# Second SwiGLU product in a written-down order: plain part last, operands stored split, first operands and weights fetched during the first product

## The chip, the cores and the metric

The kernel runs on one core of a Trainium2 chip. The metric is the device time of one execution in microseconds (us); several executions are timed and the median is taken. The engines of the core are TensorE (PE, with its weight loads PEld), VectorE (DVE), ScalarE (ACT), GpSimd (POOL) and SyncE (SP). SP issues nearly all DMA transfers of this kernel, in one queue, in the order in which the program writes them.

## What is computed

One inference step of a decoder with two layers, for a prompt of 1024 tokens and 32 sample tokens, all in fp32, D_MODEL 1024, D_FF 2816. Layer 0 mixes tokens with sliding-window attention, layer 1 with a recurrent block. Both layers end in the same SwiGLU part, which is what the change is about:

```
def swiglu(h, w_in, w_out):
    g, u = jnp.split(h @ w_in, 2, axis=-1)
    return (jax.nn.silu(g) * u) @ w_out
...
xp = xp + swiglu(rms_norm(xp, ffn_norm[layer]), w_ffn_in[layer], w_ffn_out[layer])
```

Below, "the first product" is `h @ w_in` with the SiLU gate behind it, and "the second product" is the multiplication by `w_out` with its addition to x. After layer 0 comes the norm of the recurrent block, after layer 1 the final norm, whose results `y0`, `y1`, `y2` are outputs.

## The kernel before, in words

**Arithmetic.** A fp32 matmul is done as three matmuls of a split form: every operand is held as a high part (rounded) and a low part (the rest), and `mm3` (its matmuls are on L309) adds high·high, high·low and low·high. So each matrix block, weight or activation, must be split before TensorE can use it: one ACT instruction writes the high part, one DVE subtraction the low part.

**Tokens.** The 1056 tokens lie transposed (features on partitions) in three tiles of 384, 384 and 288 columns, called t = 0, 1, 2. The residual x of a tile is held in two SBUF tiles of four feature blocks each (`x[t][0]` for blocks 0 to 3, `x[t][1]` for 4 to 7).

**First product.** D_FF is cut into 22 blocks f. For f = 0 and 1 each tile is computed plainly (`h_in`). For f = 2 to 21 the tiles 0 and 1 are computed together by `seven`, a Strassen-like scheme with seven block products in place of eight (84 matmuls of 384 columns), and tile 2 plainly by `h_in` (48 matmuls of 288 columns). During this the residual x lies in DRAM (`xd`), to make room. The hidden activations go to DRAM too: for every odd f, `keep_pair` forms the sums that the second product needs, splits six blocks and stores the high and low part of each (12 DMAs to `od`, L897 and L898). Each of these stores waits for its ACT and DVE instruction, and everything behind it in SP's queue waits with it.

**Second product.** It has a plain part, for the hidden blocks 0 and 1 (`h_out`, 144 matmuls), and 20 units (`unit`), for 5 chunks c of four hidden blocks times 4 pairs mp of output blocks. A unit is again seven products for tiles 0 and 1, in banks A, B and Dk, 42 matmuls of 384 columns, and for tile 2 24 plain matmuls of 288 columns. A unit needs nine stored operands of its chunk (b11, b21, b22, t1 to t4, and two for tile 2), a split weight block w, and the split sums ws of that weight (`Mix` on POOL, four instructions on L156 to L159, then `MixSums`). Every product that ends is added to x by DVE (`add`, L1022); a bank that goes on accumulating waits for the DVE instruction that has just read it.

**Order before.** TensorE's and SP's instructions stay in program order; ACT, DVE and POOL are ordered by a scheduler. `ffn_phase` (L838) builds a list of items; `drive` (L283) runs it, and after each item prepares what comes next in the list of needs as far as there is room. Room is scarce: 18 SBUF slots in one pool and 6 in another (`hs`) hold normalized inputs, sums, x and operands; six slots hold weights. In the second product the order before is: reload x into SBUF (`reload`, called after block f = 18), rest of the first product, plain part (`outs`), 20 units (`mixed`), of which those of the last chunk leave out tile 2, and last the tile 2 part of that chunk, with the norm of tiles 0 and 1 between (`rest`). The operands of the first chunk are fetched when the slots of the first product are free, during the plain part.

Of the kernel before, what the change touches and what calls it, by code (L numbers as in the profile page):

```python
# [9 lines left out]
OP = mybir.AluOpType  # L10
# [56 lines left out]
class Weight:  # L67


    def __init__(self, src, ext=False, place=None):  # L70
        self.src, self.ext, self.place, self.t, self.slot, self.raw = src, ext, place, None, None, None

    def prep(self, k, early=False):
        nc = k.nc
        ok = [s for s in k.wslots.free if self.ext or s[0] is k.gw]
        raw = ok and (self.place() if self.place else k.gw.tile([P, 1024], F32, name=k.nm("raw"), tag="raw", bufs=NRAW))
        if not raw:
            return False
        self.raw = raw
        self.slot = ok[0]  # L80
        k.wslots.free.remove(self.slot)
        nc.sync.dma_start(raw, self.src)
# [42 lines left out]
class Hidden:  # L125


    def __init__(self, hd, ch, t, slots, pool):
        self.hd, self.ch, self.tile, self.slots, self.pool, self.t, self.slot = hd, ch, t, slots, pool, None, None

    def prep(self, k):
        if not self.slots.free:
            return False
        W = WID[self.tile]
        self.slot = self.slots.get()
        raw = k.gw.tile([P, 2, W], F32, name=k.nm("raw"), tag="raw", bufs=NRAW)
        k.nc.sync.dma_start(raw, self.hd[self.ch, self.tile])
        self.t = self.pool().tile([P, 2, 2, WMAX], F32R, name=k.nm("h"), tag=self.slot)
        k.split(self.t[:, :, 0, :W], self.t[:, :, 1, :W], raw)
        return True  # L140

    def free(self, k):
        self.slots.put(self.slot)


class Mix:


    def __init__(self, w):
        self.w, self.t = w, None  # L150

    def prep(self, k):
        r = self.w.raw
        a, b, c, d = (r[:, i * 256:(i + 1) * 256] for i in range(4))
# [5 lines left out]
        self.t = r  # L160
        return True


class MixSums:


    def __init__(self, w):
        self.w, self.t, self.slot = w, None, None

    def prep(self, k):  # L170
        if not k.wslots.free:
            return False
        self.slot = k.wslots.get()
        self.t = self.slot[0].tile([P, 2, 1024], F32R, name=k.nm("w"), tag=self.slot[1])
# [1353 lines left out]
```

## Time and profile before

| | us |
|---|---|
| median of 3 runs (2188.15 to 2189.56) | 2188.75 |
| the profiled execution, its own time | 2185.0 |
| span in its trace | 2183.2 |
| PE busy in the span | 2129.7 (98%) |
| DVE busy | 1494.8 (68%) |
| ACT busy | 1010.0 (46%) |
| POOL busy | 243.0 (11%) |

The span of the trace leaves out 1.8 us of the profiled execution's time; the medians of the timed runs are 3.75 us above that execution. PE's busy time counts a matmul from its issue to its modelled end, so that a stream of matmuls without a gap is 100% busy whatever its rate; what matters is where PE is not busy, and which wait ends there.

### The profile page before, as it was taken

The page shows a single profiled execution, that of the slowest core. Times are in us where ns is not written, and L with a number is a line of the kernel's source. Part 1 is how long each engine was busy: PE and PEld are TensorE (multiplying, and loading weights), DVE is VectorE, ACT ScalarE, POOL GpSimd, SP SyncE. Part 2 cuts the span into 40 slices and gives each one's busy share as a digit, 9 for nine tenths or more (in the row PEclk, how much of TensorE's full clock was granted, in tenths as well). Part 3 has the DMA queues.
Part 4 walks back from the last instruction along what each step waited for, and adds up shares of the span by engine and source line. Part 5 has one row for each costly group of instructions (what it writes and reads, how often), then busy time and mean ns, then how long its engine had stood idle before and what let it go on. Part 6 is the DMA issues. An engine that isn't in the chain of part 4 may idle for free.

```text
span 2183.2 us, 35146 instructions
## 1 busy us (share of the span) xinstructions
PE 2129.7 (98%) x13608; PEld 2097.9 (96%) x13608; DVE 1494.8 (68%) x2936; ACT 1010.0 (46%) x1835; POOL 243.0 (11%) x328
## 2 busy tenths in 40 slices
PE   9999999999999999999999989999999999999997
PEld 9899989999999999999999989999999999999996
DVE  6877786756656666566776788787656666676666
ACT  5666655434444443112258887754444444422123
POOL 1223230000000001133100000000000000024222
PEclk9999999999999999999999999999999999999998
DMA  5332334323243355856112123441343343685442
GB/s 193 101 105 79 121 119 157 98 103 132 101 153 123 125 205 182 317 232 228 50 58 67 60 68 116 136 167 65 113 156 119 114 149 124 222 320 199 187 157 80
DMA packets 129135, 305.77 MB, mean 140 GB/s; under 512 B 13960, under 2 KB 82120, under 8 KB 128968
## 3 DMA queue, kind: packets, MB, share of 16 engines
q1 hardware_dynamic: 128208, 303.21, 39.9%
q8 instruction: 106, 1.74, 0.3%
q14 instruction: 61, 0.50, 0.1%
q10 hardware_dynamic: 760, 0.33, 0.1%
HBM read 220.99 MB, written 84.49 MB: 140 GB/s over the span
## 4 chain that ended last, share of the span: by engine, by line
PE 79%; DVE 10%; ACT 4%; DMA 4%; POOL 2%; issue 2%; SPq 0%; POOLq 0%; DVEq 0%; ACTq 0%
PE mm L309 75%; DVE w L88 2%; DMA o<-od 2%; DVE x L1022 1%; ACT w L84 1%; PE pt L628 1%; DVE w L348 1%; PE s L580 1%; DVE s L598 1%; DVE xn L348 1%; ACT s L605 1%; ACT w L347 0%; DVE x L423 0%; DMA raw<-in_wz 0%; POOL x L1384 0%
## 5 line engine op out<-in xcount | busy, mean ns | idle before, releaser
L309 PE MATMUL mm<-xn,w 128*128 128x384 f32 (+1 forms) x5808 | 927.0, 318 | 9.3 <-DVE w L88 3.8
L309 PEld LDWEIGHTS mm<-xn,w 128*128 128x128 f32 x5808 | 902.1, 188 | 14.2 <-DVE w L88 4.5
L309 PE MATMUL mm<-o,w 128*128 128x384 f32 (+1 forms) x2640 | 430.1, 323 | 11.8 <-DVE x L1022 8.8
L309 PEld LDWEIGHTS mm<-o,w 128*128 128x128 f32 x2640 | 420.7, 188 | 19.8 <-DVE x L1022 15.4
L88 DVE TENSOR_TENSOR w<-raw,w 128x1024 fp32r<-128x1024 f32 x246 | 300.0, 1225 | 131.6 <-ACT w L84 130.3
L84 ACT ACTIVATE w<-raw 128x1024 fp32r<-128x1024 f32 x248 | 261.3, 1056 | 199.2 <-PE mm L309 59.6
L309 PE MATMUL mm<-T,w 128*128 128x384 f32 x1920 | 351.5, 338 | 1.0 <-ACT sg L990 0.5
L309 PEld LDWEIGHTS mm<-T,w 128*128 128x128 f32 x1920 | 338.8, 188 | 1.8 <-ACT sg L990 1.1
L1022 DVE TENSOR_TENSOR x<-mm,x 128x384 f32<-128x384 f32 (+1 forms) x416 | 213.3, 531 | 134.2 <-PE mm L309 133.3
L156 POOL TENSOR_TENSOR raw<-raw 128x256 f32<-128x256 f32 x40 | 30.8, 771 | 1191.6 <-DMA raw<-in_wz 462.1
L347 ACT ACTIVATE w<-raw 128x1024 fp32r<-128x1024 f32 x40 | 42.5, 1062 | 259.8 <-PE mm L309 134.3
L620 POOL TENSOR_SCALAR s<-s,sm 128x256 f32<-128x256 f32 (+1 forms) x128 | 83.5, 669 | 210.2 <-DVE sm L618 96.3
L309 PE MATMUL mm<-att,w 128*128 128x384 f32 (+1 forms) x576 | 97.5, 325 | 0.0
L309 PEld LDWEIGHTS mm<-att,w 128*128 128x128 f32 x576 | 91.7, 188 | 1.9
L309 PE MATMUL mm<-y,w 128*128 128x384 f32 (+1 forms) x576 | 93.5, 322 | 0.0
L309 PEld LDWEIGHTS mm<-y,w 128*128 128x128 f32 x576 | 92.4, 188 | 0.0
L605 ACT ACTIVATE s<-s,sm 128x256 f32<-128x256 f32 (+1 forms) x128 | 61.7, 483 | 46.4 <-DVE sm L602 46.4
L364 ACT ACTIVATE sq<-x 128x384 f32<-128x384 f32 (+1 forms) x105 | 51.0, 491 | 56.9 <-DVE x L1022 39.6
L895 ACT ACTIVATE hi<-e 128x384 fp32r<-128x384 f32 x80 | 41.8, 522 | 69.7 <-DVE e L1013 33.7
L117 DVE TENSOR_TENSOR w<-raw,w 128x1024 fp32r<-128x1024 f32 x40 | 48.9, 1223 | 35.9 <-ACT w L115 35.8
L348 DVE TENSOR_TENSOR w<-raw,w 128x1024 fp32r<-128x1024 f32 x40 | 49.6, 1240 | 19.9 <-ACT w L347 19.7
L997 ACT ACTIVATE sg<-sg 128x384 f32<-128x384 f32 x40 | 21.0, 525 | 90.8 <-DVE sg L996 90.8
(211 smaller groups left out, 2367.4 us busy)
## 6 DMA issues: line engine op xcount, KB each, us to landing
o<-od SPq DMA_DIRECT2D x70, 768.0 KB, 9.4
od<-hi SPq DMA_DIRECT2D x140, 192.0 KB, 2.0
raw<-in_wg SPq DMA_DIRECT2D x44, 512.0 KB, 4.1
raw<-in_wu SPq DMA_DIRECT2D x44, 512.0 KB, 5.1
raw<-in_wz SPq DMA_DIRECT2D x40, 512.0 KB, 7.8
od<-e SPq DMA_DIRECT2D x80, 192.0 KB, 2.0
raw<-in_wq SPq DMA_DIRECT2D x24, 512.0 KB, 3.6
raw<-in_wo SPq DMA_DIRECT2D x24, 512.0 KB, 3.6
```

The lines of the kernel that those rows point to most:

```text
L84: nc.scalar.activation(self.t[:, 0, :], raw, AF.Copy)
L88: nc.vector.tensor_tensor(self.t[:, 1, :], raw, self.t[:, 0, :].bitcast(F32), OP.subtract)
L117: tt(d[:, 1, :], g, d[:, 0, :].bitcast(F32), OP.subtract)
L156: tt(d, c, d, OP.add)
L309: mm = lambda *a, **k: self.nc.tensor.matmul(*a, skip_group_check=more, **k)
L347: nc.scalar.activation(hi, src, AF.Copy)
L348: nc.vector.tensor_tensor(lo, src, hi.bitcast(F32), OP.subtract)
L364: nc.scalar.activation(sq[:, :W], self.xview(t, kb), AF.Square)
L605: nc.scalar.activation(s[:, j, :N], s[:, j, :N], AF.Exp, bias=sm[:, 1, j:j + 1], accum_out=sm[:, 3, j:j + 1])
L620: nc.gpsimd.tensor_scalar(s[:, j, :N], s[:, j, :N], sm[:, 4, j:j + 1], 1.0, op0=OP.mult, op1=OP.mult)
L895: nc.scalar.activation(hi.bitcast(F32R), src, AF.Copy)
L1022: tt(x, ps[:, :WID[t]], x, OP.add)
```

## The change

It concerns the second product of both layers, and small things beside it.

1. The plain part moves from before the units to behind them (`h_out`, tiles 0, 1, 2), and gives the norms of tiles 0 and 1 their place: their steps are called inside `h_out` of tiles 1 and 2 at chosen output blocks m. All 20 units now have the same form, with tile 2 in them.
2. The hidden blocks 0 and 1 are stored split, as two parts (`keep`), where before they were stored whole and split after the load.
3. What the second product needs first is fetched during the first: `lead` is woven between the last four items of the first product. y are the two items of f = 20 (`seven`, then tile 2), z those of f = 21.
4. `reload` of x moves from behind f = 18 to behind `seven` of f = 21, and takes the halves x[0][0], x[1][0], x[2][0] first.
5. In the units the loads, splits and adds come at written places: `steps[0]` behind the third product, `steps[1]` behind the fourth. There DVE's adds and the two splits are pinned to program order. `drive` no longer skips ahead to operands; a gate holds back the next phase's weights.
6. The small instructions between the sum of squares and the spread of the norm get a high priority. Of the eight stores of `y2`, four are issued by ACT.

The core of the diff:

```diff
-    def unit(w, ws, o, mp, fin, hh=None):
-        b11, b21, b22, t1, t2, t3, t4 = o
+    def unit(w, ws, o, mp, steps):
+        b11, t3, b21, t2, h0, h1, t4, t1, b22 = o
...
         prod(B, w, 1, b21, True)
-        add(0, m0, B, fin)
+        add(0, m0, B)
+        steps[0]()
         prod(A, ws, 0, t2, False)
         add(0, m1, A)
-        if hh:
-            plain(w, hh, m0, False)
+        steps[1]()
+        plain(w, (h0, h1), m0)
         prod(Dk, w, 3, t4, False)
...
     def reload():
         for t in range(NT):
             self.xt[t] = [self.act_tile([P, 4, WMAX], F32, "x") for _ in range(2)]
-            for i in range(2):
+        for i in range(2):
+            for t in range(NT):
                 nc.sync.dma_start(self.xt[t][i][0][:, :, :WID[t]], self.xd[t][:, 4 * i:4 * i + 4, :])
...
+        lead = [[lambda: fetch(0, 0, 6)], [lambda: do(0, "load")],
+                [lambda: do(0, "parts"), lambda: do(0, "sums"), lambda: do(1, "load")],
+                [reload, lambda: fetch(0, 6, 9), lambda: do(1, "parts"), lambda: do(2, "load")], [lambda: pin(True)],
+                [lambda: pin(False)]]
...
+            def s0(u=u, c=c, mp=mp):
+                if mp < 3 and c + 1 < NCH:
+                    fetch(c + 1, 3 * mp, 3 * mp + 3)
+                if mp < 3 and c + 1 == NCH:
+                    assert H[mp].prep(self)
+                do(u + 1, "sums")
+                do(u + 3, "load")
+                gate.open = u == n - 1
+            st = (s0, lambda u=u: do(u + 2, "parts"))
...
+        steps = [{}, {2: n0[1:2], 5: n0[3:4]}, {1: n1[1:2], 4: n1[3:4]}]
...
-        for f in range(NPL, NF):
+        for f in range(NPL, NF - 2):
             L += blocks(f)
-            if f == NF - 4:
-                L.append(reload)
-        p = outs()
-        m, q = mixed()
-        L += p
-        for i, x in enumerate(m):
+        y, z = blocks(NF - 2), blocks(NF - 1)
+        L += lead[0] + [y[0]] + lead[1] + [y[1]] + lead[2] + [z[0]] + lead[3] + [z[1]] + lead[4]
+        for i, x in enumerate(units):
...
-        L += [q[0]] + n0[1:2] + [q[1]] + n0[3:] + [q[2]] + n1[1:2] + [q[3]] + n1[3:]
+        L += lead[5] + p[:2] + n0[4:] + [p[2]] + n1[4:]
```

In it `load` starts the DMA of a weight block, `parts` splits it and then mixes it in place on POOL, and `sums` splits the mixed block; n0 and n1 are the steps of the norms of tiles 0 and 1 ([1] the sum over partitions, [3] the spread, [4:] the application).

**First place: SP's queue at the end of the first product of layer 0, before.** The first rows are the last stores of `keep_pair` for f = 21 (`od`, from `hi` and from `e` or `t`); x has long been loaded.

```order
L898 DMA od_4823<-e_1162_8909 128x384
L897 DMA od_4824<-hi_9256 128x384
L898 DMA od_4824<-t_9227 128x384
L195 DMA o_9314<-od_4782 128x1536
L195 DMA o_9316<-od_4783 128x1536
L195 DMA o_9318<-od_4784 128x1536
L195 DMA o_9320<-od_4785 128x1536
L195 DMA o_9322<-od_4786 128x1536
L195 DMA o_9324<-od_4787 128x1536
L195 DMA o_9326<-od_4788 128x1536
L195 DMA o_9328<-od_4789 128x4x288
L195 DMA o_9330<-od_4790 128x4x288
```

The same place in the change, from the same three stores on; `x` from `xd` is the reload, the three `o` are t4, t1 and b22 of the first chunk, `raw` from `in_wz` is the weight block of the third unit.

```order
L894 DMA od_4823<-e_1168_8933 128x384
L893 DMA od_4824<-hi_9251 128x384
L894 DMA od_4824<-t_9222 128x384
L965 DMA x_9256<-xd_71 128x1536
L965 DMA x_9258<-xd_72 128x1536
L965 DMA x_9260<-xd_73 128x4x288
L965 DMA x_9257<-xd_71 128x1536
L965 DMA x_9259<-xd_72 128x1536
L965 DMA x_9261<-xd_73 128x4x288
L202 DMA o_9268<-od_4788 128x1536
L202 DMA o_9270<-od_4785 128x1536
L202 DMA o_9272<-od_4784 128x1536
```

Six of the nine operands have left this place (they are now ahead of the stores of f = 20), the six loads of x have come to it, and both still stand behind the twelve stores of f = 21. The next row of the change is `L149 DMA raw_9281<-in_wz 128x1024`.

**Second place: DVE in the first unit of layer 0, before.** `x` from `mm` are the adds, `w` from `raw` the low parts of weights; `w_9406` is the split of the third unit's weight block, `raw_9404`.

```order
L1022 TENSOR_TENSOR x_8680<-mm_9567,x_8680 128x384
L1022 TENSOR_TENSOR x_8684<-mm_9569,x_8684 128x384
L1022 TENSOR_TENSOR x_8680<-mm_9568,x_8680 128x384
L1022 TENSOR_TENSOR x_8680<-mm_9567,x_8680 128x384
L1022 TENSOR_TENSOR x_8688<-mm_9598,x_8688 128x288
L1022 TENSOR_TENSOR x_8680<-mm_9569,x_8680 128x384
L1022 TENSOR_TENSOR x_8684<-mm_9567,x_8684 128x384
L88 TENSOR_TENSOR w_9406<-raw_9404,w_9406 128x1024
L1022 TENSOR_TENSOR x_8688<-mm_9626,x_8688 128x288
```

And in the change; `w_9385` is the split of the third unit's weight block, `raw_9281`, and bank A is `mm_9343`.

```order
L1014 TENSOR_TENSOR x_9256<-mm_9343,x_9256 128x384
L1014 TENSOR_TENSOR x_9258<-mm_9345,x_9258 128x384
L1014 TENSOR_TENSOR x_9256<-mm_9344,x_9256 128x384
L135 TENSOR_TENSOR w_9373<-raw_9118,w_9373 128x1024
L1014 TENSOR_TENSOR x_9256<-mm_9343,x_9256 128x384
L135 TENSOR_TENSOR w_9385<-raw_9281,w_9385 128x1024
L1014 TENSOR_TENSOR x_9260<-mm_9392,x_9260 128x288
L1014 TENSOR_TENSOR x_9256<-mm_9345,x_9256 128x384
L1014 TENSOR_TENSOR x_9258<-mm_9343,x_9258 128x384
L1014 TENSOR_TENSOR x_9260<-mm_9420,x_9260 128x288
L1014 TENSOR_TENSOR x_9258<-mm_9343,x_9258 128x384
```

The split of the third unit's weight has moved ahead of three adds of the first unit, the third of which (bank A to x of tile 1) TensorE's seventh product waits for.

**Third place: POOL at the end of the kernel, before.** `rc` is the inverse root of the norm of a tile, tiles 0, 1, 2 in turn; `x` times `rs` is the final norm applied to tile 1 (eight blocks) and to two blocks of tile 2.

```order
L377 TENSOR_TENSOR rc_21860<-rc_21860,mhalf 128x3
L377 TENSOR_TENSOR rc_21959<-rc_21959,mhalf 128x3
L377 TENSOR_TENSOR rc_22032<-rc_22032,mhalf 128x3
L1384 TENSOR_TENSOR x_19141<-x_19141,rs_22014 128x384 x4
L1384 TENSOR_TENSOR x_19142<-x_19142,rs_22014 128x384 x4
L1384 TENSOR_TENSOR x_19145<-x_19145,rs_22047 128x288
L1384 TENSOR_TENSOR x_19146<-x_19146,rs_22047 128x288
```

And in the change:

```order
L379 TENSOR_TENSOR rc_21833<-rc_21833,mhalf 128x3
L379 TENSOR_TENSOR rc_21941<-rc_21941,mhalf 128x3
L1384 TENSOR_TENSOR x_19722<-x_19722,rs_21995 128x384 x4
L1384 TENSOR_TENSOR x_19723<-x_19723,rs_21995 128x384 x4
L379 TENSOR_TENSOR rc_22046<-rc_22046,mhalf 128x3
L1384 TENSOR_TENSOR x_19724<-x_19724,rs_22061 128x288
L1384 TENSOR_TENSOR x_19725<-x_19725,rs_22061 128x288
```

The inverse root of tile 2 now stands behind the eight multiplications of tile 1.

More of the change, by code (lines that the diff above doesn't have):

```diff
@@ L75, in prep @@
         ok = [s for s in k.wslots.free if self.ext or s[0] is k.gw]
[L76 to L77 removed]
+        if not ok:
             return False
[L79 removed]
         self.slot = ok[0]
         k.wslots.free.remove(self.slot)
+        raw = self.raw = k.gw.tile([P, 1024], F32, name=k.nm("raw"), tag="raw", bufs=NRAW)
         nc.sync.dma_start(raw, self.src)
@@ L122, in free, with __init__, fill, load @@
             k.wslots.put(s)
[L125 to L140, printed above, removed]
-    def free(self, k):
[L143 to L154, printed above, removed]
+class Part:
+    def __init__(self):
+        self.t, self.slot = None, None
+    def fill(self, k, raw):
+        nc, pin = k.nc, k.tc.keep_in_program_order if k.pinned else lambda x: x
+        self.slot = k.wslots.get()
+        self.t = self.slot[0].tile([P, 2, 1024], F32R, name=k.nm("w"), tag=self.slot[1])
+        pin(nc.scalar.activation(self.t[:, 0, :], raw, AF.Copy))
+        pin(nc.vector.tensor_tensor(self.t[:, 1, :], raw, self.t[:, 0, :].bitcast(F32), OP.subtract))
+    def free(self, k):
+        k.wslots.put(self.slot)
+class Mixed:
+    def __init__(self, src):
+        self.src, self.w, self.s = src, Part(), Part()
+    def load(self, k):
+        self.raw = k.gw.tile([P, 1024], F32, name=k.nm("raw"), tag="raw", bufs=NRAW)
+        k.nc.sync.dma_start(self.raw, self.src)
+    def parts(self, k):
+        self.w.fill(k, self.raw)
+        a, b, c, d = (self.raw[:, i * 256:(i + 1) * 256] for i in range(4))
         tt = k.nc.gpsimd.tensor_tensor
@@ L159, in prep, with sums, __init__, parts @@
         tt(b, b, a, OP.subtract)
[L160 to L168, printed above, removed]
-    def prep(self, k):
[L171 to L174, printed above, removed]
-        k.split(self.t[:, 0, :], self.t[:, 1, :], self.w.raw)
-        return True
-    def free(self, k):
-        k.wslots.put(self.slot)
+    def sums(self, k):
+        self.s.fill(k, self.raw)
+class Whole:
+    def __init__(self, src):
+        self.src, self.w = src, Part()
+    load = Mixed.load
+    def parts(self, k):
+        self.w.fill(k, self.raw)
+    def sums(self, k):
+        pass
+class Gate:
+    def __init__(self):
+        self.t, self.open = None, False
+    def prep(self, k):
+        return self.open
 class Operand:
@@ L846, in ffn_phase @@
         T, HD_, OD = {}, {}, {}
-        late = []
+        n0, n1 = after
+        pools = [(lambda: self.hp, hs), (lambda: self.gp, self.slots)]
         NCH = (NF - 2) // 4
@@ L924, in h_in @@
             u = self.proj(wu, self.xn[t], W)
-            flush()
             if last:
@@ L1033, in h_out, with plain @@
                              h[:, c, 0, :W], h[:, c, 1, :W], c == 0, c == 1)
-                add(t, m, ps)
-        def plain(w, hh, m, fin):
+                x = self.xview(t, m)
+                with tc.high_priority(PRI):
+                    tt(x, ps[:, :W], x, OP.add)
+                if l == 1 or t < 2:
+                    self.square(t, m)
+                for fn in steps.get(m, ()):
+                    fn()
+        def plain(w, hh, m):
             W = WID[2]
@@ L1092, in blocks @@
                     Item(lambda a, b: h_in(a, b, f, 2, last=f == NF - 1), w, w)]
-        def outs():
-            w = [Weight(I[f"wd{l}"][k], True) for k in range(2)]
-            h = [Hidden(HD_, 0, t, hs, lambda: self.hp) for t in range(NT)]
-            return [Item(lambda a, b, h, t=t: h_out(a, b, h, t), w + [h[t]],
-                         (w if t == 2 else []) + [h[t]]) for t in range(NT)]
-        def third():
-            if "raw" not in T:
-                if not hs.free:
-                    return None
-                T["raw"] = hs.free.pop()
-            t = self.hp.tile([P, 4 * WMAX], F32, name=self.nm("raw"), tag=T["raw"])
-            return t[:, :1024]
```

115 lines of the change are left out of this document (50 added, 65 removed).

## The prediction

> **What bounds the kernel now.** I read the page first (busy times, then the costliest groups), then who waits for whom on PE, then PE's busy time over the two second products, then the timelines of PE and SP around their starts and ends.
>
> ```profile
> PE 2129.7 (98%) x13608; PEld 2097.9 (96%) x13608; DVE 1494.8 (68%) x2936; ACT 1010.0 (46%) x1835; POOL 243.0 (11%) x328
> ...
> L88 DVE TENSOR_TENSOR w<-raw,w 128x1024 fp32r<-128x1024 f32 x246 | 300.0, 1225 | 131.6 <-ACT w L84 130.3
> L84 ACT ACTIVATE w<-raw 128x1024 fp32r<-128x1024 f32 x248 | 261.3, 1056 | 199.2 <-PE mm L309 59.6
> ...
> L1022 DVE TENSOR_TENSOR x<-mm,x 128x384 f32<-128x384 f32 (+1 forms) x416 | 213.3, 531 | 134.2 <-PE mm L309 133.3
> ```
>
> PE works without a break nearly everywhere: 53.5 us of 2183.2 are not busy. The change leaves the number of matmuls as it is, so it can only move PE's waits and the stretch behind its last matmul. A weight's split costs 1.06 us on ACT and 1.22 us on DVE, an add to x 0.53 us.
>
> PE's longest waits, by what ended them (us, times, longest),
>
> ```profile
> PE mm L309 <- DVE x L1022: 8.8, 18, 2.5
> ```
>
> and PE's busy time from the first to the last matmul of the units, layer 0 and layer 1:
>
> ```profile
> 880.40:1103.90 223.50, 216.62 (x1340) 212.14 (x1338) 147.52 (x249) 50.84 (x61) 55.05 (x74) 1.00 0.51 191
> 1943.20:2164.30 221.10, 216.20 (x1340) 212.20 (x1339) 147.36 (x250) 54.92 (x70) 59.85 (x75) 1.00 0.48 182
> ```
>
> The units lose 6.9 and 4.9 us to waits, mostly for an add that a weight's split holds up on DVE. That is all that a better order inside them can win: 11.8 us.
>
> PE around the start of the second product of layer 0 (T and xn belong to the first product, h to the plain part, o to the units):
>
> ```profile
> 838.50 4.39 PE L309 MATMUL mm<-T,w 128*128 128x384 f32 x24
> 842.72 2.24 PE L309 MATMUL mm<-xn,w 128*128 128x384 f32 x12
> ...
> 849.03 8.60 PE L309 MATMUL mm<-xn,w 128*128 128x384 f32 x60
> 857.47 23.15 PE L309 MATMUL mm<-h,w 128*128 128x384 f32 x144
> 880.46 1.22 PE L309 MATMUL mm<-o,w 128*128 128x384 f32 x6
> ```
>
> From start to start, 24 matmuls of 384 columns take 842.72 - 838.50 = 4.22 us, so 0.176 each. The row at 849.03 holds the last 12 of `seven` for f = 21 and 48 of tile 2. I call the end of `seven` E: 849.03 + 12 x 0.176 = 851.1. Tile 2 then covers 6.3 us and the plain part 23.0 us, before the first unit needs its operands.
>
> SP in the same stretch, from the last store of f = 21 on:
>
> ```profile
> 866.80 1.41 SPq L898 DMA_DIRECT2D od<-t  x1
> 868.30 5.29 SPq L195 DMA_DIRECT2D o<-od  x9
> ```
>
> The store leaves at E + 15.7, and only then the nine operands, at E + 17.2. For f = 19 a row of PE and one of SP:
>
> ```profile
> 806.79 10.71 PE L309 MATMUL mm<-xn,w 128*128 128x384 f32 x72
> ```
> ```profile
> 820.87 0.44 SPq L898 DMA_DIRECT2D od<-t  x1
> ```
>
> There `seven` ended at 806.79 + 2.1 = 808.9, and the last store left 12.0 us behind it.
>
> How long the nine operands take, from the chain of waits, their sizes, and the load of the DMA engines meanwhile:
>
> ```profile
> 873.06 14.08 DMA o<-od
> ```
> ```profile
> o<-od SPq DMA_DIRECT2D x70, 768.0 KB, 9.4
> ...
> o<-od SPq DMA_DIRECT2D x20, 576.0 KB, 13.1
> ...
> x<-xd SPq DMA_DIRECT2D x8, 768.0 KB, 6.5
> ...
> x<-xd SPq DMA_DIRECT2D x4, 576.0 KB, 10.9
> ```
> ```profile
> 870.00:890.00 20.00, 18.83 (x120) 18.09 (x119) 10.86 (x21) 1.85 (x2) 0.00 (x0) 1.00 1.02 407
> ```
>
> Seven of 768 KB and two of 576 KB need 887.1 - 868.3 = 18.8 us from the first issue to the last landing. The DMA engines are full (share 1.02), at 407 GB/s: 1.9 us for 768 KB, 1.3 us for a weight block of 512 KB.
>
> **The change part by part.**
>
> *Start of the units, the term that decides.* The plain part no longer stands between E and the units: they begin at E + 6.3. In SP's queue the twelve stores of f = 21 still come first, then six loads of x (four of 768 KB, two of 576 KB), then t4, t1 and b22: by the sizes above exactly the bytes of the nine operands of before. What was hidden under 29.3 us now lies under 6.3.
>
> When does SP get past the stores? Before, at E + 17.2, with splits of hidden blocks and weights among the stores' instructions; at f = 19, at 12.0. Those splits go, but two weight splits come, and each high part's buffer waits for an earlier store to land. I take E + 11, with 17 as one end; the other end is DVE's own work on these blocks, 13 instructions (five sums, six low parts, two of tile 2) at the price of this row:
>
> ```profile
> L896 DVE TENSOR_TENSOR e<-e,hi 128x384 fp32r<-128x384 f32 x16 | 9.1, 586 | 2.0 <-ACT hi L895 2.0
> ```
>
> 13 x 0.59 = 7.6 us. From E + 11, counted back from the last landing at + 18.8 by 1.9 us per 768 KB and 1.4 per 576 KB: x of tile 0 lands at E + 15.3, t4 at E + 26.0, b22 at E + 29.8, the third weight block at E + 31.1.
>
> A matmul of 288 columns takes (1096.04 - 1092.77) / 24 = 0.136 us:
>
> ```profile
> 1092.77 3.43 PE L309 MATMUL mm<-o,w 128*128 128x288 f32 x24
> 1096.04 0.22 PE L390 MATMUL mm<-idr,rh 128*128 128x128 f32 x1
> ```
>
> PE in the first unit: three products of 6 x 0.176 = 1.06 us end at E + 9.5. The fourth goes on in bank A and needs the first add, so x: 15.3 + 0.5 = E + 15.8, a wait of 6.3. It and half of tile 2 (12 x 0.136 = 1.6) bring PE to E + 18.5; the fifth needs t4: 26.0, a wait of 7.5. Fifth, sixth and the other half of tile 2 bring it to E + 29.7. The seventh needs the add of bank A, which on DVE stands behind the split of the third weight block: 31.1 + 1.06 + 1.22 and three adds of 0.53 make E + 35.0, a wait of 5.3. Sum: 19.1 us per layer, **+38.2**. With SP free at 7.6 or 17 it is 15.7 or 25 per layer. From then on a unit of 42 x 0.176 + 24 x 0.136 = 10.7 us needs a quarter of a chunk's operands and one weight block, 18.8 / 4 + 1.3 = 6 us of DMA, so I expect no further wait.
>
> What the clock does after a wait is in PE's rows and the stretch of the change of layers:
>
> ```profile
> 1107.67 0.47 PE L390 MATMUL mm<-idr,rh 128*128 128x128 f32 x1 [3.76 <-DVE rh L378]
> ...
> 1110.16 20.13 PE L309 MATMUL mm<-xn,w 128*128 128x384 f32 x107
> ```
> ```profile
> 1100.00:1120.00 20.00, 15.35 (x86) 14.93 (x85) 18.34 (x41) 10.13 (x19) 0.85 (x1) 0.83 0.17 52
> ```
>
> *Clock.* Behind a wait of 3.8 us the granted clock of these 20 us is 0.83, and 107 matmuls take 20.1 us where 107 x 0.176 = 18.8: 1.3 us lost. The waits above are longer; what two of them cost is covered by the next wait, the third is not: 2 x 1.3, **+2.6** (0 to 6). [...]
>
> *Inside the units.* The written order puts each add ahead of the split that used to hold it up, and gives banks tile 2's 1.6 us as cover in the last chunk too: the waits of before go, **-11.8** (at least -9). What is late next is nothing on DVE: a unit has 9 adds and 2 splits, about 7 of 10.7 us.
>
> *Change of layers.* Before, 4.7 us of waits in the 20 us from 1100 on, and 1.3 of clock. In the change the sums and spreads of both norms lie inside `h_out`, with high priority. But DVE still has 16 instructions of the norm of tile 0 and six adds to do after the second sum, 22 x 0.53 = 11.7 us against six blocks of tile 2, 6 x 6 x 0.136 = 4.9, of matmuls left, and the recurrent block's first matmuls follow it: I leave 2 us of wait. **-4** (0 to -6). Inside `h_out` DVE has an add and a sum of squares per 1.06 us of PE, so each sum over partitions may wait half a us: **+1**.
>
> *Tail.* Rows of before:
>
> ```profile
> 2160.85 3.43 PE L309 MATMUL mm<-o,w 128*128 128x288 f32 x24
> ```
> ```profile
> 2167.87 0.85 POOL L377 TENSOR_TENSOR rc<-rc,mhalf 128x3 f32<-128x3 f32 x1 [3.56 <-DVE rc L376]
> 2168.69 9.16 POOL L1384 TENSOR_TENSOR x<-x,rs 128x384 f32<-128x384 f32 x10
> ...
> 2172.43 2.64 DVE L1386 SCALAR_TENSOR_TENSOR x<-x,vec,mm 128x288 f32<-128x288 f32 x6 [1.79 <-ACT rs L397]
> ```
>
> The last product ends at 2164.3, the span 18.9 us later, with POOL's ten multiplications (0.92 us each) as the last link. In the change eight of them start some 2 us before PE's end, since the spread of tile 1 lies three output blocks (3 x 6 x 0.136 = 2.4 us) ahead of it, so they end about 6 us behind it. The inverse root of tile 2 now queues behind them, 3 us later than before, but then only two are left: root at + 6.8, DVE's last product as before 6.4 us later (2175.07 - 2168.72), a store and its landing, which I put at 2: about + 15. **-4** (0 to -6).
>
> *At nothing:* the split storing of blocks 0 and 1 adds six ACT and six DVE instructions per layer early in the first product, where PE's stream hides them (3.5 us of DVE if it did not); the six early operands take 10.5 us of DMA during two items of 21 us each, and the weights of f = 21 stand ahead of them in SP's queue.
>
> Sum: 38.2 + 2.6 - 11.8 - 4 + 1 - 4 = +22.0. The profiled execution took 2185.0 us (1.8 outside its span), so 2207.0 by its measure; its median stands 3.75 above: 2188.75 + 22.0 = **2210.75 us**.
>
> **The rivals.**
>
> 1. *The queue is free in time* (faster). If the twelve stores left by E, because nothing but their own splits stands in ACT and DVE, every landing above comes 11 us earlier and a layer loses 8.1 us at the start: 2188.75 + 22.0 - 22.0 = 2188.75. That is the point from which it decides; at E - 3 it gives about 2183. For it: the blocks' splits have less beside them than before. Against it: the last at + 12.0 and + 15.7, and 7.6 us of DVE work. Faster needs this or a landing that my sizes don't give: 0.14. Between, within 0.2% (4.4 us, about what a measurement of this kernel can tell from no change): 0.06.
> 2. *The start's delay stays.* If the third and fourth weight blocks land late too, since each is queued behind three operands, DVE's pinned order stops PE again in the second unit, by a block's 18.8 - 11 = some 5 us per layer: 2221 or more. For it: share 1.02 for 40 us. Against it: 6 of 10.7 us of DMA are enough for a unit. 0.06.
> 3. *The change does not fetch early enough to matter, nor late enough to hurt*: SP free at 7.6 and all gains at their best ends: 31.4 - 11.8 - 6 - 6 = +8, 2196. 0.14.
>
> My forecast has the rest, 0.60. In all: faster 0.14, same 0.06, slower 0.80. The range leaves out rival 2 (0.06) and most of rival 1: 2188 to 2221.
>
> **What would show it.** Right: three waits of PE in the first unit of each layer, ended by the add of x, by DMA of o, and by an add of bank A with a weight's split ahead of it; SP's x loads about 11 us behind `seven`; units without waits afterwards; a shorter tail. Wrong: x loaded within a few us of E, or PE in step through the first unit. If the first unit takes less than 19 us (10.7 and 8.1), the sign of the forecast falls.

## The result, and the profile after

| | before | changed |
|---|---|---|
| median of 4 runs each (range), us | 2188.45 (2186.22 to 2189.56) | 2211.30 (2210.47 to 2212.06) |
| the profiled execution, us | 2185.0 | 2210.95 |
| span in its trace, us | 2183.2 | 2208.9 |
| mean granted clock | 0.99 | 0.983 |

The changed kernel takes 1.0106 of the time of before (95% interval 1.0088 to 1.0123): 22.85 us more by the medians, where +22.0 was forecast. By the spans it is 25.7 us more, mostly since the profiled execution of before lay 3.4 us under its median and that of the change only 0.35. L numbers are now those of the changed kernel: L310 the matmuls, L1014 the add to x in a unit, L1026 that in `h_out`, L366 the sums of squares.

First who waits for whom on PE: the total, the number of waits, the longest.

```profile
PE mm L310 <- DVE x L1014: 24.6, 4, 9.9
PE mm L310 <- DMA o<-od: 10.4, 2, 5.3
PE mm L373 <- DVE acc L366: 10.0, 3, 7.5
```

Before, the add to x ended 18 waits of 2.5 us at most. Now it ends four long ones, two in each layer, and the operands `o` end one in each. PE around the start of the units, layer 0:

```profile
847.76 8.60 PE L310 MATMUL mm<-xn,w 128*128 128x384 f32 x60
...
868.54 4.78 PE L310 MATMUL mm<-o,w 128*128 128x384 f32 x18 [9.00 <-DVE x L1014]
878.45 5.98 PE L310 MATMUL mm<-o,w 128*128 128x384 f32 x24 [5.12 <-DMA o<-od]
887.01 28.16 PE L310 MATMUL mm<-o,w 128*128 128x384 f32 x155 [2.58 <-DVE x L1014]
```

E, the end of `seven` for f = 21, is 847.76 + 12 x 0.176 = 849.87. Behind it come tile 2, three products, and then the three forecast waits. The fourth product starts at 868.54, E + 18.7; the fifth, which needs t4, at E + 28.6; the seventh, which needs the add of bank A, at E + 37.1. The rows also show the clock: 18 matmuls (6 of 384 columns, 12 of 288) take 4.78 us where 6 x 0.176 + 12 x 0.136 = 2.7 are due, the next 24 take 5.98 instead of 3.7. The granted clock of these two stretches was 0.56 and 0.62.

That the seventh product waits behind the third weight block shows on DVE, which has the block's split directly ahead of four adds (885.58 to 887.32), among them that of bank A:

```profile
884.43 1.23 DVE L135 TENSOR_TENSOR w<-raw,w 128x1024 fp32r<-128x1024 f32 x1 [11.98 <-ACT w L134]
```

Layer 1:

```profile
1919.20 8.60 PE L310 MATMUL mm<-xn,w 128*128 128x384 f32 x60
...
1940.90 4.53 PE L310 MATMUL mm<-o,w 128*128 128x384 f32 x18 [9.92 <-DVE x L1014]
1950.74 5.76 PE L310 MATMUL mm<-o,w 128*128 128x384 f32 x24 [5.32 <-DMA o<-od]
1959.56 25.68 PE L310 MATMUL mm<-o,w 128*128 128x384 f32 x157 [3.06 <-DVE x L1014]
```

E is 1919.20 + 2.11 = 1921.31, and the same three products start at E + 19.6, 29.4 and 38.3. What SP does meanwhile in layer 0, with the last of the twelve stores, the x tiles, and t4, t1 and b22:

```profile
862.95 0.32 SPq L894 DMA_DIRECT2D od<-t  x1
863.37 3.49 SPq L965 DMA_DIRECT2D x<-xd  x6
866.90 1.60 SPq L202 DMA_DIRECT2D o<-od  x3
```

The x loads leave at E + 13.5, behind the stores. Then the units from the seventh product of the first one to the end of the twentieth, in each layer, and the first 6 us of that stretch in layer 0 (length; busy time of PE, PEld, DVE, ACT, POOL; granted clock, DMA share, GB/s):

```profile
887.01:893.00 5.99, 5.99 (x19) 5.99 (x20) 1.43 (x3) 1.28 (x2) 1.72 (x3) 0.50 1.02 423
887.01:1091.00 203.99, 203.99 (x1261) 203.99 (x1262) 130.43 (x209) 38.31 (x38) 51.85 (x71) 0.98 0.56 199
1959.56:2160.50 200.94, 200.94 (x1260) 200.94 (x1261) 130.43 (x209) 37.35 (x37) 51.83 (x71) 1.00 0.51 185
```

PE is busy for the whole of both: the waits of 6.9 and 4.9 us that the units had before are gone. The same work takes 3.05 us more in layer 0, since the clock was still at 0.50 behind the third wait there; in layer 1 it was at 1.00. At the change of layers, PE's rows with a wait:

```profile
1111.50 0.83 PE L373 MATMUL mm<-ones,acc 128*128 128x1 f32 x6 [0.45 <-DVE acc L366]
...
1120.90 1.15 PE L310 MATMUL mm<-xn,w 128*128 128x384 f32 x5 [0.36 <-DVE xn L349]
1122.45 0.44 PE L310 MATMUL mm<-xn,w 128*128 128x384 f32 x1 [0.40 <-ACT xn L348]
1123.26 7.07 PE L310 MATMUL mm<-xn,w 128*128 128x384 f32 x39 [0.37 <-DVE xn L349]
```

1.6 us of waits in all, and the 39 matmuls of the last row run at the full rate (39 x 0.176 = 6.9), where before there were 4.7 us and a granted clock of 0.83; from 1100 to 1120 it is now 1.00. Last the tail, all engines, with PE's last 18 matmuls of the plain part in the first row:

```profile
2187.72 2.61 PE L310 MATMUL mm<-o,w 128*128 128x288 f32 x18
...
2188.49 9.00 POOL L1384 TENSOR_TENSOR x<-x,rs 128x384 f32<-128x384 f32 x8 [4.11 <-ACT rs L399]
...
2189.62 1.18 DVE L366 TENSOR_TENSOR acc<-acc,sq 128x288 f32<-128x288 f32 x1
2190.72 0.44 DVE L1026 TENSOR_TENSOR x<-mm,x 128x288 f32<-128x288 f32 x1
...
2192.26 5.55 DVE L366 TENSOR_TENSOR acc<-acc,sq 128x288 f32<-128x288 f32 x5
...
2197.86 1.44 PE L373 MATMUL mm<-ones,acc 128*128 128x1 f32 x6 [7.53 <-DVE acc L366]
```

The last of them ends at 2190.33 and the span 18.6 us later, against 18.9 before. While POOL multiplies tile 1, DVE's sums of squares of tile 2 take about 1.1 us each, and PE waits 7.53 us for them.

### The profile page after: what moved, and what is told of

The parts are those of the page before. It is cut to its first block, busy times and chain, and to the rows that moved or that the text cites. A ratio compares the mean times of both kernels' runs of the same rounds, so it can differ in the third digit from the quotient of the medians.

```text
span 2208.9 us, 35229 instructions
## 1 busy us (share of the span) xinstructions
PE 2133.2 (97%) x13608; PEld 2107.0 (95%) x13608; DVE 1496.0 (68%) x2934; ACT 1008.7 (46%) x1841; POOL 237.1 (11%) x328
## 4 chain that ended last, share of the span: by engine, by line
PE 82%; DVE 8%; ACT 4%; DMA 3%; issue 1%; POOL 1%; SPq 0%; ACTq 0%; DVEq 0%; POOLq 0%
PE mm L310 79%; DMA raw<-in_wz 1%; DVE w L87 1%; PE pt L630 1%; ACT w L83 1%; PE s L582 1%; DVE s L600 1%; ACT s L607 1%; DVE acc L366 1%; DMA x<-xd 1%; DVE xn L349 0%; PE mm L373 0%; DVE pr L349 0%; ACT w L134 0%; DVE xs L425 0%
## 5 line engine op out<-in xcount | busy, mean ns | idle before, releaser
L310 PE MATMUL mm<-xn,w 128*128 128x384 f32 (+1 forms) x5808 | 927.2, 318 | 11.7 <-DVE w L87 3.8
L310 PEld LDWEIGHTS mm<-xn,w 128*128 128x128 f32 x5808 | 900.8, 188 | 18.2 <-DVE w L87 4.7
L310 PE MATMUL mm<-o,w 128*128 128x384 f32 (+1 forms) x2928 | 482.6, 327 | 35.0 <-DVE x L1014 24.6
L310 PEld LDWEIGHTS mm<-o,w 128*128 128x128 f32 x2928 | 478.7, 192 | 36.8 <-DVE x L1014 25.7
L310 PE MATMUL mm<-T,w 128*128 128x384 f32 x1920 | 351.3, 338 | 0.3 <-ACT sg L983 0.3
L310 PEld LDWEIGHTS mm<-T,w 128*128 128x128 f32 x1920 | 338.9, 188 | 0.6 <-ACT sg L983 0.6
L1014 DVE TENSOR_TENSOR x<-mm,x 128x384 f32<-128x384 f32 x360 | 191.5, 534 | 158.0 <-PE mm L310 143.5
L155 POOL TENSOR_TENSOR raw<-raw 128x256 f32<-128x256 f32 x40 | 29.4, 736 | 1213.8 <-DVE w L135 1213.8
L310 PE MATMUL mm<-att,w 128*128 128x384 f32 (+1 forms) x576 | 97.2, 325 | 0.0
L310 PE MATMUL mm<-y,w 128*128 128x384 f32 (+1 forms) x576 | 93.5, 323 | 0.0
L310 PEld LDWEIGHTS mm<-att,w 128*128 128x128 f32 x576 | 91.4, 188 | 1.9
L310 PEld LDWEIGHTS mm<-y,w 128*128 128x128 f32 x576 | 92.4, 188 | 0.0
L892 DVE TENSOR_TENSOR t<-t,hi 128x384 fp32r<-128x384 f32 x60 | 33.4, 556 | 45.6 <-ACT hi L891 44.4
```

Of the source, the lines that this page charges most:

```text
L310: mm = lambda *a, **k: self.nc.tensor.matmul(*a, skip_group_check=more, **k)
L892: tt(src.bitcast(F32R), src, hi, OP.subtract)
L1014: tc.keep_in_program_order(tt(x, ps[:, :WID[t]], x, OP.add))
```

## The experiments

The theory: the twelve stores of f = 21, which wait for DVE and ACT, hold SP until E + 13.5, and what stands behind them in SP's queue then takes its bytes' time; these places in the queue set all three waits. The main rival: the written order itself, with its pinned adds and splits, makes the first unit slow, whatever is loaded when. For each kernel the table has the ratio to the kernel before with its interval, and how far behind E the seventh product starts in layer 0 (the changed kernel: 37.1).

| experiment | median, us | ratio to before | seventh product |
|---|---|---|---|
| e1_swap | 2212.74 | 1.0123 (1.0109 to 1.0136) | E + 37.0 |
| e2_halves | 2203.95 | 1.0086 (1.0072 to 1.0100) | E + 32.0 |
| e3_x_ahead | 2197.49 | 1.0051 (1.0038 to 1.0063) | E + 30.2 |
| e4_tail | 2211.33 | 1.0115 (1.0101 to 1.0129) | E + 37.3 |
| e7_ahead | 2192.25 | 1.0021 (1.0012 to 1.0031) | |
| e4b_dve | 2209.55 | 1.0104 (1.0090 to 1.0118) | |
| e5_split_later | 2206.46 | 1.0093 (1.0079 to 1.0107) | |
| e6_fill | 2214.41 | 1.0125 (1.0111 to 1.0139) | E + 38.5 |
| e8_queue | 2178.56 | 0.9967 (0.9954 to 0.9979) | E + 23.3 |
| e9_all | 2178.24 | 0.9962 (0.9949 to 0.9976) | |
| e10_combined | 2189.16 | 1.0015 (1.0007 to 1.0024) | |

The first four stood beside runs of the kernel before with a median of 2185.65 us, the next four 2186.96, the last three 2186.4; so the ratios are compared, not the medians. e4_tail turned out to leave the order as it was, and so is a second measurement of the changed kernel, 1.0115.

### Exchange what is late: x early, the operands late (e1_swap)

```diff
-            lead = [[lambda: fetch(0, 0, 6)], ...
+            lead = [[reload], ...
-                    [reload, lambda: fetch(0, 6, 9), ...
+                    [lambda: fetch(0, 0, 9), ...
```

> The x tiles are loaded early, in the place of the six early operands, and all nine operands of the first chunk are loaded late, where the changed kernel has the reload of x. The bytes behind the stores of f=21 stay much the same. Theory (the SP queue is blocked until about 13.5 us after the end of seven for f=21, and what stands behind the stores then takes its bytes' time): the first matmuls wait for the operands instead of the adds for x, the time stays within 2 us of the changed kernel's 2211.3 us, and the three waits on the add of x turn into waits on operands. Rival (the written order with its pinned adds costs the time by itself, whatever is loaded late): the adds of x no longer wait, yet the gaps between the first products stay waits on DVE, at 2211 us as well; or, if x alone was at fault, clearly less, 2195 us or below.

PE's two longest waits at the start, layer 0:

```profile
868.61 8.29 PE L310 MATMUL mm<-o,w 128*128 128x384 f32 x30 [11.30 <-DMA o<-od]
...
887.82 27.35 PE L310 MATMUL mm<-o,w 128*128 128x384 f32 x158 [3.82 <-DVE x L1014]
```

Now no product can start before its operand lands, and the seventh stands at the same place as in the changed kernel. The time is the same (1.0123 against 1.0115 and 1.0106). It doesn't matter what stands behind the stores; that it stands there does. The first wait is no longer for an add of x, so it isn't the adds that cost.

### Fewer bytes ahead of t4 (e2_halves)

```diff
-            for i in range(2):
-                for t in range(NT):
-                    nc.sync.dma_start(self.xt[t][i][0]...)
+            halves(0)
+
+        def halves(i):
+            for t in range(NT):
+                nc.sync.dma_start(self.xt[t][i][0]...)
...
-                    [reload, ..., lambda: do(2, "load")], ...
+                    [reload, ..., lambda: do(2, "load"), lambda: halves(1)], ...
```

> Only the first halves of the x tiles are reloaded ahead of the operands; the second halves go behind the third weight block. That takes 2.16 MB, some 5.3 us at the rate of the transfers in this place, from ahead of t4, t1, b22 and the third weight block. Theory (each of the first waits is set by the place of its transfer in SP's queue): the first wait stays, since the first half comes as before, the waits for t4 and for the third weight block's split shrink by about 5 us together in each layer: 2200 us (2197 to 2205). Rival (the waits are set by the engines' written order and the transfers would be there anyway): 2211 us, no change. Rival (every microsecond of queue time counts once for each wait): below 2195 us.

PE, layer 0:

```profile
867.32 6.19 PE L310 MATMUL mm<-o,w 128*128 128x384 f32 x24 [9.12 <-DVE x L1016]
873.89 2.90 PE L310 MATMUL mm<-o,w 128*128 128x384 f32 x18 [0.38 <-DMA o<-od]
880.55 13.21 PE L310 MATMUL mm<-o,w 128*128 128x384 f32 x66 [3.75 <-DVE x L1016]
895.48 19.76 PE L310 MATMUL mm<-o,w 128*128 128x384 f32 x120 [1.72 <-DVE x L1016]
```

The first wait stays, that for t4 falls from 5.12 to 0.38, and a late second half makes a new one of 1.72. The seventh product comes 5.1 us earlier, of which 1.7 are given back: 3.4 in layer 0, and 4.4 in layer 1 (5.5 less 1.1), 7.8 in all. Against e4_tail, timed beside the same runs of the kernel before, the ratio falls by 0.0029, 6.3 us. The waits move with the places of their transfers in the queue.

### Two x tiles ahead of the stores (e3_x_ahead)

```diff
             def post():
+                if f == NF - 1:
+                    reload((0, 1))
...
-                    [reload, lambda: fetch(0, 6, 9), ...
+                    [lambda: reload((2,)), lambda: fetch(0, 6, 9), ...
```

> The reload of x tiles 0 and 1 is issued ahead of the last twelve stores of f=21 instead of behind them; tile 2 stays where it is. Theory (the stores, which wait for DVE, hold SP until 13.5 us after the end of seven for f=21, and x behind them is what the first adds wait for): the first wait of about 9 us goes, and the operands t4, t1, b22 come earlier by the time of the four x transfers; some 10 us less a layer, 2191 us (2186 to 2198). Rival (the second late thing, t4 or the third weight block, takes the place of the first wait): about 5 us less a layer or nothing, 2201 to 2211 us.

PE, layer 0:

```profile
848.68 8.60 PE L310 MATMUL mm<-xn,w 128*128 128x384 f32 x60
...
862.75 4.34 PE L310 MATMUL mm<-o,w 128*128 128x384 f32 x18 [2.30 <-DVE x L1016]
872.24 6.28 PE L310 MATMUL mm<-o,w 128*128 128x384 f32 x24 [5.14 <-DMA o<-od]
881.03 34.20 PE L310 MATMUL mm<-o,w 128*128 128x384 f32 x203 [2.52 <-DVE x L1016]
```

The first wait falls from 9.00 to 2.30 us; t4 and the split are late as before, but 7 us earlier behind E. 14 us less (1.0051 against 1.0115): inside the theory's range but at its far end, between its 20 us and the rival's 10, as the wait for t4 stayed.

### TensorE kept busy instead of waiting (e6_fill)

```diff
-            if last:
-                self.freeall(self.xn[t])
...
+            def fill():
+                ps = self.bank()
+                for i in range(130):
+                    x = self.xn[2][i % 4][0]
+                    nc.tensor.matmul(ps[:, :WID[2]], x[:, 0, 0, :P], x[:, 1, 0, :WID[2]], start=True, stop=True)
+                self.freeall(self.xn[2])
...
-                    ... [lambda: pin(True)],
+                    ... [fill, lambda: pin(True)],
```

> 130 matmuls whose result nobody reads (they leave the computation as it is) are put ahead of the first unit in each layer: 130 x 0.136 us, some 17.7 us of TensorE a layer, 35 us in all. Theory (the start of the units waits some 20 us a layer for transfers and what follows them, not for TensorE): they lie in those waits, and the time rises by far less than 35 us, to 2212 (2206 to 2222); it may even fall a little if the clock doesn't drop. Rival (TensorE's own work sets the start, the gaps are small beside it): 35 us more, 2246 us.

PE, layer 0 (L1108 are the added matmuls):

```profile
855.83 17.28 PE L1108 MATMUL mm<-xn 128*128 128x288 f32 x130
872.95 5.99 PE L310 MATMUL mm<-o,w 128*128 128x384 f32 x36
...
888.05 27.25 PE L310 MATMUL mm<-o,w 128*128 128x384 f32 x153 [3.76 <-DVE x L1012]
```

Some 35 us of TensorE work (17.28 us a layer) cost about 3 us (1.0125 against 1.0106 and 1.0115). The seventh product stands at E + 38.5, where it stood at 37.1 without them. So the start of the units is empty time of TensorE, and the lower clock behind the first two waits costs little by itself: without these waits the products are faster (the 36 matmuls behind the added ones take 5.99 us, where 24 x 0.176 + 12 x 0.136 = 5.9 are due), and wait the longer for the third weight block (3.76 us).

### Everything ahead of the stores (e7_ahead)

```diff
             def post():
+                if f == NF - 1:
+                    T["ahead"]()
...
+            def ahead():
+                reload()
+                fetch(0, 6, 9)
+                do(2, "load")
...
-                    [reload, lambda: fetch(0, 6, 9), lambda: do(1, "parts"), lambda: do(2, "load")], ...
+                    [lambda: do(1, "parts")], ...
```

> All that the changed kernel issues behind the last twelve stores of f=21 (six x transfers, t4, t1, b22, the third weight block) is issued ahead of them; SP then waits only for seven for f=21 to end, and the stores follow. Theory (the place behind the stores is what makes the first products wait): the waits for the first add of x, for t4 and for the third weight block go, except some 2 us behind DVE's work for the stores; 5 to 8 us less a layer than with two of the three x tiles ahead, which gave 2197.5: 2184 us (2179 to 2190), so that the change as a whole is no slower than the kernel before. Rival (the stores, now behind ten transfers, come late and hold ACT and DVE, whose adds the next products wait for): 2192 us or more.

All engines, layer 0: ACT's high part for one of the stores, and PE's fourth product:

```profile
866.42 0.52 ACT L891 ACTIVATE hi<-e 128x384 fp32r<-128x384 f32 x1 [11.28 <-DMA od<-hi]
...
869.79 18.96 PE L310 MATMUL mm<-o,w 128*128 128x384 f32 x108 [9.74 <-DVE x L1016]
```

Here the rival has it: 2192.25. SP's part is as intended, t4 and the split are no longer waited for. But the stores are now issued behind ten transfers: the first leaves SP at 853.99, and ACT gets a high part's buffer back only at 866.42. ACT stands 11.28 us for it, DVE behind ACT 8.83, and the add of x, pinned behind DVE's low parts, ends the one long wait that is left in each layer (9.74 and 9.90 us). The change as a whole is still 0.2% slower.

### The tail (e4_tail, e4b_dve)

```diff
-        L += lead[5] + p[:2] + n0[4:] + [p[2]] + n1[4:]
+        L += lead[5] + p[:2] + n0[4:] + [p[2]] + (n1[4:] if l == 0 else [])
+        self.n1rest = n1[4:]
...
+            f2 = self.final_steps(2)
...
-                       self.final_steps(2) + [endF1])
+                       f2[:4] + self.n1rest + f2[4:] + [endF1])
```

> In layer 1 alone, the eight multiplications by which POOL applies the last norm to tile 1 are put behind the root and spread of tile 2. Theory (they run beside DVE's last adds and squares of tile 2, which take 1.17 us each there instead of 0.45 us, and TensorE waits 7.5 us for the sum of squares): DVE's adds and squares return to about 0.45 us, the wait of 7.5 us falls to about 3 us, and the end comes 2 to 3 us earlier if tile 1's output is not late in its turn: 2208.5 us. Rival (the squares are slow for another reason, or tile 1's output now ends last): 2211 us or up to 4 us more.

2211.33, no change: POOL is ordered by the scheduler and kept the multiplications at the same place, 0.77 us behind the start of PE's last 18 matmuls (in the changed kernel 2188.49 - 2187.72, the same). So this said nothing of the cause. The second edit also moves them to another engine (and places them behind f2[:2]):

```diff
-                nc.gpsimd.tensor_tensor(x, x, self.rs[t][:, :W], OP.mult)
+                (nc.vector if t == 1 else nc.gpsimd).tensor_tensor(x, x, self.rs[t][:, :W], OP.mult)
```

> In the last norm alone, tile 1's eight multiplications are made by DVE, between and behind tile 2's sums of squares, where the changed kernel has them on POOL beside these sums. (The experiment that only wrote them later in the program moved nothing: the trace has them at the same place on POOL.) Theory (DVE's sums take 1.1 us instead of 0.45 us because POOL multiplies at the same time): they return to about 0.45 us, TensorE's wait of 7.5 us for them falls to about 4.5 us, as four multiplications of some 0.55 us come between, and the end is 3 us earlier: 2208 us (2207 to 2209.5). Rival (the sums are slow whatever POOL does): they stay at 1.1 us, four multiplications come on top, and the end is 2 us later: 2213 us.

PE and DVE in its tail:

```profile
2187.16 2.75 PE L310 MATMUL mm<-o,w 128*128 128x288 f32 x18
...
2188.74 0.45 DVE L366 TENSOR_TENSOR acc<-acc,sq 128x288 f32<-128x288 f32 x1
...
2194.18 1.35 PE L373 MATMUL mm<-ones,acc 128*128 128x1 f32 x6 [4.26 <-DVE acc L366]
```

With POOL idle the sums take 0.45 us, though DVE now does the multiplications too (0.55 us each); PE waits 4.26 us, and the span of 2205.7 ends 15.8 us behind the last product, not 18.6. The trace shows the cause and 2.8 us; the timed ratios (1.0104 against 1.0115 and 1.0106) are too near each other to confirm the 2.8 us by themselves.

### The split of the third weight block (e5_split_later)

```diff
-                st = (s0, lambda u=u: do(u + 2, "parts"))
+                st = (s0, lambda u=u: do(u + 2, "parts") if u else None)
...
+                if u == 0:
+                    items[-1].tail = lambda: do(2, "parts")
```

> The splitting of the third weight block, which is pinned on DVE ahead of the add that frees a bank in the first unit, is put behind the first unit. Theory (this place alone costs the third wait of the start, 2.6 and 3.1 us in the two layers; the second unit then has its weights later): at most 5.5 us less, 2206 us (2205 to 2209). Rival (the second unit waits for the same weights, or its own products do): 2211 us, no change.

PE, layer 0, from the fifth product on:

```profile
878.39 14.26 PE L310 MATMUL mm<-o,w 128*128 128x384 f32 x72 [4.72 <-DMA o<-od]
893.72 21.60 PE L310 MATMUL mm<-o,w 128*128 128x384 f32 x132 [1.07 <-DVE x L1014]
```

The third wait is gone, a later one of 1.07 takes its place. 1.0093 against 1.0106 and 1.0115, some 3 to 5 us less, as expected; the intervals overlap, so it is the trace that shows the wait moved, not the time alone.

### The operands on a queue of their own, and sums of the edits (e8_queue, e10_combined, e9_all)

```diff
             def post():
+                if f == NF - 1:
+                    reload((0, 1), nc.sync)
...
                 nc.scalar.activation(g1, A[:, :WMAX], AF.Silu)
+                if f == NF - 1:
+                    reload((2,), nc.scalar)
+                    T["ahead"]()
                 tt(u2, u2, sg, OP.mult)
...
+            T["ahead"] = lambda: fetch(0, 6, 9, nc.scalar)
...
-                    [reload, lambda: fetch(0, 6, 9), lambda: do(1, "parts"), ...
+                    [lambda: do(1, "parts"), ...
```

> x tiles 0 and 1 go on SP ahead of the last twelve stores of f=21, as in the experiment that gave 1.0051 of the kernel before; x tile 2, t4, t1 and b22 are issued on ACT's queue as soon as seven for f=21 ends, beside the stores on SP; the third weight block stays behind the stores. Theory (the operands are late only because they stand behind the stores, and on a queue of their own they needn't hold the stores up as they did when all stood ahead of them on SP): the waits for t4 of some 5 us go in both layers, and about 8 us of the whole time: 1.0015 of the kernel before, 2190 us (2184 to 2194). Rival (the 3.5 MB take the transfers' time from the stores, whose buffers ACT and DVE then wait for, as they did with all ahead): a wait on DVE's add of 5 us or more takes their place, no change or slower, 1.005 or more (2197).

All engines, layer 0 (E is 847.32 + 2.11 = 849.43):

```profile
847.32 8.60 PE L310 MATMUL mm<-xn,w 128*128 128x384 f32 x60
...
849.68 0.96 ACTq L965 DMA_DIRECT2D x<-xd  x2
...
857.28 0.53 ACT L891 ACTIVATE hi<-e 128x384 fp32r<-128x384 f32 x1 [3.47 <-DMA od<-hi]
...
863.16 9.19 PE L310 MATMUL mm<-o,w 128*128 128x384 f32 x42 [4.07 <-DVE x L1019]
...
872.74 39.59 PE L310 MATMUL mm<-o,w 128*128 128x384 f32 x245 [0.38 <-DVE x L1019]
```

No wait for t4 any more. ACT's longest wait for a store's buffer is 3.47 us (6.8 in all), where it was 11.28 with all transfers on SP, and PE 4.07 and 0.38 us in all (3.77 and 1.61 in layer 1); the seventh product is at E + 23.3. The kernel takes 0.9967 of before: the written order is faster than the kernel before once its first operands aren't queued behind the stores. The expectation was 8 us under e3_x_ahead, it became 18: the third wait shrank too, which fits the third weight block no longer having 3.5 MB ahead of it in its queue (ACT begins its split 4.1 us behind its issue, 864.94 to 869.07, where in e3_x_ahead it took 9.9, 867.45 to 877.37), and one slow stretch a layer is left: the 42 matmuls behind the first wait take 9.19 us in layer 0 and 8.12 in layer 1, where 18 x 0.176 + 24 x 0.136 = 6.4 are due, and the 76 behind the second in layer 0 take 12.52, where 12.4 are due. Against e3_x_ahead, which has the same two x tiles ahead of the stores, what differs is that x of tile 2, t4, t1 and b22 have another queue and with it another place in the order; no run here measures the two apart.

The other two kernels only put edits together that are shown above: e10_combined has e3_x_ahead with the late split and tile 1's multiplications on DVE, e9_all has e8_queue with them.

> x tiles 0 and 1 ahead of the stores, everything else of the start where the changed kernel has it, with the third weight block's split behind the first unit and tile 1's last multiplications on DVE. Theory (the gains add up: 1.0051 of the kernel before by the x tiles, 2.5 us a layer by the split, 3 us by the tail): 8 us under the x tiles alone: 1.0015 of the kernel before, 2190 us (2186 to 2193). Rival (with x there earlier the split is no longer what the bank waits for): 3 us under it, 1.0037, 2195 us.

> The same queues, and besides the third weight block's split behind the first unit and tile 1's last multiplications on DVE. Theory (the three costs are apart from each other): 5 and 3 us less than with the queues alone: 0.998 of the kernel before, 2182 us (2177 to 2190), faster than both kernels. Rival (the split's wait was cover for something that comes next, or the start is limited by DVE's work for the stores): 2 to 3 us less than with the queues alone, by the tail only.

e10_combined came out as expected, 1.0015: the three gains add up. In e9_all they did not show in the time: 0.9962 against 0.9967 is no difference. The traces say why for the split: e8_queue has third waits of 0.38 and 1.61 us, and e9_all has later ones of 1.07 us in each layer in their place, so nothing was left to win. The tail's gain is in the trace (PE's waits for the sums of squares fall from 10.0 to 6.9 us, the profiled span from 2178.5 to 2175.6), but the medians do not show it. Both are faster than the kernel before; which of them is best stays open.

## Why the prediction was right

**The start of the units** was the term that decides, and its mechanism is shown: SP's queue behind the stores (e1_swap, e2_halves, e3_x_ahead), for the third wait with the pinned split behind its transfer (e5_split_later), and TensorE empty meanwhile (e6_fill). In us behind E:

| | forecast | layer 0 | layer 1 |
|---|---|---|---|
| SP past the stores | 11 | 13.5 | 13.5 |
| fourth product (x) | 15.8 | 18.7 | 19.6 |
| fifth product (t4) | 26.0 | 28.6 | 29.4 |
| seventh product (bank A) | 35.0 | 37.1 | 38.3 |
| late by, against 15.9 without waits | 19.1 | 21.2 | 22.4 |

The step that was 2.5 us off is the time of the stores, E + 11, and it carries through the table nearly unchanged: the sizes of the transfers behind it were right. (By the prediction's own figures x of tile 0 lands at E + 15.6, not 15.3; the next waits cover the difference.) What fills the time until E + 13.5, all engines, layer 0:

```profile
852.25 1.09 DVE L1006 TENSOR_TENSOR e<-e,xs 128x384 f32<-128x384 f32 x1
...
853.01 0.94 POOL L157 TENSOR_TENSOR raw<-raw 128x256 f32<-128x256 f32 x1
...
855.30 0.55 DVE L910 TENSOR_TENSOR t<-e,t 128x384 f32<-128x384 f32 x1
...
859.31 0.52 ACT L891 ACTIVATE hi<-t 128x384 fp32r<-128x384 f32 x1 [1.92 <-DMA od<-hi]
...
860.74 1.04 ACT L134 ACTIVATE w<-raw 128x1024 fp32r<-128x1024 f32 x1
...
862.37 0.56 DVE L892 TENSOR_TENSOR t<-t,hi 128x384 fp32r<-128x384 f32 x1 [1.04 <-ACT hi L891]
```

Two things show. POOL forms the sums of the second weight block until 854.96, and four of DVE's five sums beside it take 0.73 to 1.09 us; the fifth, behind POOL's end, takes 0.55. That is 1.7 us. Then ACT waits 1.92 us for a buffer of a high part whose store is under way, and does a weight's split of 1.04 us ahead of the last high part, for which the last low part waits. That POOL is the cause of the first is argued from these rows and from the tail (e4b_dve), not tried at this place; nor was the order on ACT.

**The clock** was put at 1.3 us a layer behind the third wait, 2.6 in all, with the cost behind the first two covered by the next wait. The first part came out in sum but not by layer: 3.05 us in layer 0, none in layer 1. The second is right: in layer 0 the products behind the first two waits took about (4.78 - 2.7) + (5.98 - 3.7) = 4.3 us more, so that only 16.7 of the 21.2 us show as waits, and e6_fill bears out that this costs little by itself.

**Inside the units** the mechanism is right, no wait of PE is left behind the first unit's start, but the size was too small. The prediction took PE's idle time, 6.9 + 4.9 = 11.8 us, for all that could be won. By the stretch of layer 1 at full clock, 19 units and a product in 200.94 us, twenty units take 210.4. Before, they took 223.5 - 1.8 and 221.1 - 1.8 us (1.8 for the norms' short matmuls between them), 11.3 and 8.9 more. So the gain was 20.2 us, and the 8.4 us that were missed lay in PE's busy time, at a granted clock of 1.00; a part may be that a wait delays PE by more than its idle time, as that of 2.46 us which ends at 936.99 of before does by 0.16 (2.75 us lie from one matmul's start to the next one's, where such a matmul takes 0.13); the rest has no cause shown. Rival 2, the next weight blocks late too, did not come; its price, "18.8 - 11 = some 5 us", is 7.8 by its own terms.

**The change of layers**: -4 forecast. Before, 4.7 us of waits and 1.3 of clock; now 1.6 at full clock: -4.4. **`h_out`**: +1 forecast. In layer 1 one sum alone cost a wait of 1.98 us, and 18 matmuls behind it took 4.16 us instead of 2.6: +3.5.

```profile
2182.42 0.83 PE L373 MATMUL mm<-ones,acc 128*128 128x1 f32 x6 [1.98 <-DVE acc L366]
2183.11 4.16 PE L310 MATMUL mm<-o,w 128*128 128x288 f32 x18
```

**The tail** is the step that failed: -4 forecast, -0.3 measured. The prediction had POOL's eight multiplications beside PE's last matmuls as free cover, and left DVE's sums of squares as fast as before. It looked for the harm in tile 2's root queued behind them on POOL; the harm was at DVE's sums ahead of that root, about 1.1 us each instead of 0.45. Without POOL beside them 2.8 us come back (e4b_dve).

The sum: 43.6 at the start, +3.05 for the clock behind it, -20.2, -4.4, +3.5, -0.3 and -1.2 for a first product that ended earlier in layer 0 (849.87 against 851.1) make +24.0, against 25.7 by the spans; 1.7 us are not assigned. So the 0.5 us between forecast and result (2210.75 and 2211.30) are luck in good part: the start, the sums inside `h_out` and the tail cost 5.4, 2.5 and 3.7 us more than forecast, the units won 8.4 us more, and the profiled execution of before lay 3.4 us under its median.

**The rivals**: the first, SP free in time, needed the stores gone by E; they went at E + 13.5. e8_queue shows that its mechanism is real when the queue is made free by another way: what decides the sign is the place of nine transfers, the six of x and the three operands.

## What to carry to other kernels

When work that used to hide transfers is moved, list what each DMA queue holds between the last thing it must wait for and the first thing that is now needed, and add up its bytes: here that gave the loss to some 3 us a layer. Loads that wait for nothing do not belong behind stores that wait for an engine; but here loads put ahead of the stores on the same queue held up the stores' buffers (ACT waited 11.28 us for one in e7_ahead), so a second queue was what helped (3.47 us in e8_queue, and 0.9967 of before). An order that removes every wait inside the steady state can still be slower by its start. And what such an order wins can be more than the idle time that a profile shows: here 20.2 us against 11.8.

## What the runs showed of the hardware

While POOL multiplies in the tail of the changed kernel, DVE's sum of two SBUF tiles (L366) takes 1.18 us, 0.88 us and then five times 1.11 us on average; in e4b_dve, with POOL idle there, it takes 0.45. DVE's add of a PSUM bank to an SBUF tile (L1026) takes 0.44 us beside POOL in the changed kernel and 0.46 in e4b_dve.
